# Row sums of a 67 MB array on one Trainium2 core: blocks of 15 rows per partition in place of 16

## The chip, the core and the metric

The kernel runs on one core of one Trainium2 chip. A core has several engines with instruction streams of their own: VectorE (DVE in the profile), ScalarE (ACT), GpSimd (POOL), TensorE (PE, unused here) and SyncE (SP), which here only issues transfers. Transfers between the chip's memory (HBM) and the core's on-chip memory, which has 128 partitions, are carried out by 16 DMA engines that work beside all of these. The metric is the device time of one execution in microseconds (us), the median of several runs. A transfer is issued by SP or by ScalarE, and whoever needs its data waits for its completion signal.

## The reference

The input is x, 32 x 512 x 1024 in float32 (67.11 MB). The output is the sum of each row of 1024 numbers, so 16384 sums:

```python
def reference(x: np.ndarray) -> np.ndarray:
    return np.sum(x, axis=-1).astype(np.float32)
```

## The kernel before

The 16384 rows are dealt out to the 128 partitions, J = 128 rows each. They are cut into eight blocks of 128 x 16 rows (8.39 MB). Within a block, partition p holds 16 rows that are neighbours in memory, so its share is one contiguous run of 64 KB, and the runs of neighbouring partitions lie 64 KB apart. `x_g` (L120) is this view of the input, `out_v` (L121) the same of the output, and `rows_from(j, n)` (L123) picks n rows of a block. The sums are collected in `sums` (L138), 128 columns for each partition.

Buffers for the loaded rows come from the pool `in` (L133), three of them, each of 16 rows and four spare numbers per partition, used in turn. A load into a buffer waits until the work that read its last contents is done. The order of instructions on each engine is the order of the program text (`manual_schedule`, L136).

`rows` (L177) does one load and its reductions: it issues the load on SP (L180), and then sums the rows in one of two ways on VectorE, and the last `n_act` rows on ScalarE. `vec` (L140) is one VectorE instruction for all rows of the load; `halves` (L153), used with `pairs=True`, is one VectorE instruction for each row, which adds the row's two halves and sums up. `act` (L166) sums one row on ScalarE, with an output in another memory that nobody reads.

The order of loads is this. First come 7 rows of the last block (L197 to L200, `FIRST` = 7), the first 7 of its 16. Then come blocks 0 to 6, of 16 rows each (L201 to L208); blocks 0 to 5 are summed by one `vec` each, block 6 by 9 `halves` and 7 `act`. The load of block 1 is held with `hold` (L145, L208) until the reduction of the first 7 rows is done, and as SP issues in order, the loads after it come later too. Then follow the rest of the last block: 6 rows, 2 rows, and its last row in two pieces of 536 and 488 numbers (L210 to L223). The pieces are summed by two `halves`; the first one's sum is placed ahead of the second piece, so that the second instruction adds it in, and a zero written at L220 makes the length even.

Two stores go out. The first, issued by ScalarE (L224), holds the sums of blocks 0 to 6, and is held back until the load of 2 rows has landed. The second, issued by SP (L227), holds the last block's 16 sums of each partition.

Three functions change the finished instruction list, and the change leaves them as they are: `issue_first_load_at_entry` (L10) moves SP's first load to the program's entry, `order_waits` (L31) sorts the waits of single instructions, and `wait_for_the_store_at_the_clear` (L55) lets the last store's wait stand at a later place of the program's end.

Of the kernel before, what the change touches and what calls it, by code (L numbers as in the profile page):

```python
# [100 lines left out]
@with_exitstack  # L101
def kernel(
    ctx: ExitStack,
    tc: tile.TileContext,
    x: bass.AP,
    out: bass.AP,
):
    nc = tc.nc
    nc.at_finalize(issue_first_load_at_entry)
    nc.at_finalize(order_waits)  # L110
    nc.at_finalize(wait_for_the_store_at_the_clear)
    fp32 = mybir.dt.float32
    P = 128
    batch, seq, dim = x.shape
    rows = batch * seq
    J = rows // P
    BIG = 16


    x_g = x.flatten_outer_dims().rearrange("(g p j) d -> g p j d", p=P, j=BIG)  # L120
    out_v = out.rearrange("b s -> (b s)").rearrange("(g p j) -> p g j", p=P, j=BIG)  # L121

    def rows_from(j, n):  # L123
        return x_g[j // BIG, :, j % BIG : j % BIG + n, :]

    last = J // BIG - 1
    FIRST = 7
    pieces = (536, 488)  # L130

    with (
        tc.tile_pool(name="in", bufs=3) as inpool,  # L133
        tc.tile_pool(name="unread", bufs=4, space=bass.MemoryType.PSUM) as upool,
        tc.tile_pool(name="stage", bufs=1) as stpool,
        tc.manual_schedule(),  # L136
    ):
        sums = stpool.tile([P, J], fp32)  # L138

        def vec(dst, src):  # L140
            return nc.vector.tensor_reduce(  # L141
                out=dst, in_=src, axis=mybir.AxisListType.X, op=mybir.AluOpType.add
            )

        def hold(inst, until, reason):  # L145
            tc.add_manual_dep(
                inst.ins,
                until.ins.name,
                mybir.DependencyInfo(mybir.DependencyClass.Sync, mybir.DependencyReason.DATA),
                reason=reason,  # L150
            )

        def halves(dst, src):  # L153
            n = src.shape[-1] // 2
            return nc.vector.tensor_tensor_reduce(  # L155
                out=src[:, :n],
                in0=src[:, :n],
                in1=src[:, n:],
                scale=1.0,
                scalar=0.0,  # L160
                op0=mybir.AluOpType.add,
                op1=mybir.AluOpType.add,
                accum_out=dst,
            )

        def act(dst, src, n):  # L166
            unread = upool.tile([P, dim], fp32)
            nc.scalar.activation(  # L168
                out=unread[:, :n],
                in_=src,  # L170
                func=mybir.ActivationFunctionType.Copy,
                accum_out=dst,
            )

        sums_of = []

        def rows(t, a, n, j, n_act, pairs=False):  # L177
            nv = n - n_act
            block = t[:, a * dim : (a + n) * dim].rearrange("p (n d) -> p n d", d=dim)
            load = nc.sync.dma_start(out=block, in_=rows_from(j, n))  # L180
            if pairs:
                for q in range(nv):
                    sums_of.append(halves(sums[:, j + q : j + q + 1], block[:, q, :]))
            else:
                sums_of.append(vec(sums[:, j : j + nv], block[:, :nv, :]))
            for q in range(nv, n):
                act(sums[:, j + q : j + q + 1], block[:, q, :], dim)
            return load

        def store(eng, g0, g1):  # L190
            return eng.dma_start(
                out=out_v[:, g0:g1],
                in_=sums[:, g0 * BIG : g1 * BIG].rearrange("p (g j) -> p g j", j=BIG),
            )


        j = last * BIG  # L197
        t = inpool.tile([P, BIG * dim + 4], fp32)
        rows(t, 0, FIRST, j, 0)
        first = sums_of[-1]  # L200
        for g in range(last):  # L201
            t = inpool.tile([P, BIG * dim + 4], fp32)
            if g < last - 1:
                load = rows(t, 0, BIG, g * BIG, 0)
            else:
                rows(t, 0, BIG, g * BIG, 7, pairs=True)
            if g == 1:
                hold(load, first, "no descriptors of later loads while the first ones start")  # L208

        t = inpool.tile([P, BIG * dim + 4], fp32)  # L210
        rows(t, FIRST, 6, j + FIRST, 2, pairs=True)
        two = rows(t, FIRST + 6, 2, j + FIRST + 6, 1, pairs=True)
        a = BIG - 1

        j += a
        c, width = pieces
        whole = t[:, a * dim + c : BIG * dim + 2]
        nc.vector.memset(whole[:, width + 1 :], 0.0)  # L220
        part = t[:, a * dim : a * dim + c]
        nc.sync.dma_start(out=part, in_=rows_from(j, 1)[:, 0, :c])  # L222
        nc.sync.dma_start(out=whole[:, 1 : width + 1], in_=rows_from(j, 1)[:, 0, c:])  # L223
        hold(store(nc.scalar, 0, last), two, "its packets come behind those of the loads")  # L224
        halves(whole[:, :1], part)
        halves(sums[:, j : j + 1], whole)
        store(nc.sync, last, last + 1)  # L227


# [28 lines left out]
```

## Time and profile before

| what | value |
|---|---|
| runs, median (lowest, highest) | 161.85 us (161.43, 162.03) |
| span of the profiled execution, first to last instruction | 160.3 us |
| total time of the profiled execution | not recorded; the median lies 1.5 us above its span |
| read from HBM | 67.11 MB, 419 GB/s over the span |
| VectorE: reductions of 16 rows, L141 | 6 of 17.22 us |
| VectorE: reduction of the first 7 rows, L141 | 7.62 us |
| VectorE: one row as halves, L155 | 14 of 0.69 us |
| ScalarE: one row, L168 | 10 of 1.01 us |
| issue of a load on SP, L180 | 0.33 us (median) |
| first load (7 rows), from issue to landing | 11.0 us |

The span is counted from the first to the last instruction, so that what lies around it (starting and finishing the program) belongs to the time of a run, but not to the span. A load's time from issue to landing holds the time that it queues behind other loads. The share of a DMA queue is the time of its packets as a share of what 16 engines have in the span; q1 holds what SP issues, q10 what ScalarE issues. In the chain of work that ended last, each step is followed back to what released it; a step named DMA is the time from a load's issue, or from the end of the piece ahead of it in the chain, to its landing.

### The profile page before, as it was taken

The page shows a single profiled execution, that of the slowest core. Times are in us where ns is not written, and L with a number is a line of the kernel's source. Part 1 is how long each engine was busy: PE and PEld are TensorE (multiplying, and loading weights), DVE is VectorE, ACT ScalarE, POOL GpSimd, SP SyncE. Part 2 cuts the span into 40 slices and gives each one's busy share as a digit, 9 for nine tenths or more (in the row PEclk, how much of TensorE's full clock was granted, in tenths as well). Part 3 has the DMA queues.
Part 4 walks back from the last instruction along what each step waited for, and adds up shares of the span by engine and source line. Part 5 has one row for each costly group of instructions (what it writes and reads, how often), then busy time and mean ns, then how long its engine had stood idle before and what let it go on. Part 6 is the DMA issues. An engine that isn't in the chain of part 4 may idle for free.

```text
span 160.3 us, 132 instructions
## 1 busy us (share of the span) xinstructions
DVE 120.6 (75%) x40; ACT 11.9 (7%) x21; POOL 0.2 (0%) x4
## 2 busy tenths in 40 slices
DVE  0029600499986999679995999949999499994955
ACT  3000000000000000000000000000000000003993
POOL 0000000000000000000000000000000000000000
DMA  8999999899799699699699699796996996996994
GB/s 300 386 491 523 392 392 523 376 409 523 327 458 523 294 491 523 262 523 523 262 523 523 262 523 441 343 523 278 507 523 262 523 523 262 523 523 264 423 384 123
DMA packets 2784, 67.18 MB, mean 419 GB/s; under 512 B 1248, under 2 KB 1376, under 8 KB 1504
## 3 DMA queue, kind: packets, MB, share of 16 engines
q1 hardware_dynamic: 1872, 67.12, 97.7%
q10 hardware_dynamic: 912, 0.06, 0.4%
HBM read 67.11 MB, written 0.07 MB: 419 GB/s over the span
## 4 chain that ended last, share of the span: by engine, by line
DMA 71%; DVE 27%; SPq 1%; issue 0%; DVEq 0%
DMA t<-in_x_dram 71%; DVE sums L141 26%; SPq L180 0%; SPq L222 0%; DVE t L155 0%; DVEq L253 0%
## 5 line engine op out<-in xcount | busy, mean ns | idle before, releaser
L141 DVE TENSOR_REDUCE sums<-t 128x16 f32<-128x16384 f32 (+1 forms) x7 | 110.9, 15848 | 33.8 <-DMA t<-in_x_dram 33.8
L168 ACT ACTIVATE unread<-t 128x1024 f32<-128x1024 f32 x10 | 10.1, 1012 | 145.3 <-DMA t<-in_x_dram 145.3
L155 DVE CUSTOM_DVE_ANT_0 t<-t 128x512 f32<-128x512 f32 (+2 forms) x16 | 9.6, 656 | 4.1 <-DMA t<-in_x_dram 4.0
L168 ACT ACTIVATION_READ_ACCUMULATOR unread<-t 128x1 f32 x10 | 1.9, 187 | 0.0
L168 ACT ACT_TABLE_LOAD x1 | 1.3, 1283 | 0.8 <-PEq L242 0.8
L155 DVE DVE_READ_ACCUMULATOR2_ANT sums<- 128x1 f32 x15 | 1.3, 84 | 0.0
L242 POOL MEMSET const-bfloat16-1.0<- 128x1 bf16 x1 | 0.1, 101 | 0.0
L242 POOL MEMSET const-uint8-127<- 128x1 uint8 x1 | 0.1, 101 | 0.0
L242 POOL MEMSET const-float32-0.0<- 128x1 f32 x1 | 0.1, 98 | 0.2 <-issue 0.2
L242 POOL MEMSET const-float32-1.0<- 128x1 f32 x1 | 0.1, 98 | 0.0
L155 DVE DVE_READ_ACCUMULATOR2_ANT t<- 128x1 f32 x1 | 0.1, 83 | 0.0
L220 DVE MEMSET t<- 128x1 f32 x1 | 0.1, 59 | 0.0
## 6 DMA issues: line engine op xcount, KB each, us to landing
t<-in_x_dram SPq DMA_DIRECT2D x1, 3584.0 KB, 11.0
t<-in_x_dram SPq DMA_DIRECT2D x1, 3072.0 KB, 29.0
t<-in_x_dram SPq DMA_DIRECT2D x1, 1024.0 KB, 31.1
t<-in_x_dram SPq DMA_DIRECT2D x1, 268.0 KB, 31.4
t<-in_x_dram SPq DMA_DIRECT2D x1, 244.0 KB, 31.4
t<-in_x_dram SPq DMA_DIRECT2D x7, 41.1
out_dram<-sums ACTq DMA_DIRECT2D x1, 56.0 KB, 2.1
out_dram<-sums SPq DMA_DIRECT2D x1, 8.0 KB, 1.4
```

The lines of the kernel that those rows point to most:

```text
L141: return nc.vector.tensor_reduce(out=dst, in_=src, axis=mybir.AxisListType.X, op=mybir.AluOpType.add)
L155: return nc.vector.tensor_tensor_reduce(out=src[:, :n], in0=src[:, :n], in1=src[:, n:], scale=1.0, scalar=0.0, op0=mybir.AluOpType.add, op ...
L168: nc.scalar.activation(out=unread[:, :n], in_=src, func=mybir.ActivationFunctionType.Copy, accum_out=dst,)
L220: nc.vector.memset(whole[:, width + 1 :], 0.0)
L242: nc = _bacc.Bacc("TRN2", target_bir_lowering=False, num_devices=1)
```

## The change

Blocks are made of 15 rows for each partition (a run of 60 KB, and runs 60 KB apart), and there are eight of them, for 120 of a partition's 128 rows. The 8 rows that are left form a last block of its own, with runs of 32 KB lying 32 KB apart, loaded as 5 rows, 2 rows and one row in the same two pieces. The early load of 7 rows goes, and with it the hold on block 1's load. Blocks 0 to 6 are summed by one `vec` each, block 7 by 9 `halves` and 6 `act`, the five rows by 4 `halves` and 1 `act`, the two rows by one of each, as they are now. Buffers have 15 rows and no spare numbers. The early store holds 120 sums of each partition, as 8 runs of 60 bytes (it was 7 runs of 64), and the last store 8 (it was 16).

```diff
-    BIG = 16
-    x_g = x.flatten_outer_dims().rearrange("(g p j) d -> g p j d", p=P, j=BIG)
-    out_v = out.rearrange("b s -> (b s)").rearrange("(g p j) -> p g j", p=P, j=BIG)
-    def rows_from(j, n):
-        return x_g[j // BIG, :, j % BIG : j % BIG + n, :]
-    last = J // BIG - 1
-    FIRST = 7
+    BIG = 15
+    blocks = J // BIG
+    REST = J - blocks * BIG
+    assert REST == 8
+    x_r = x.flatten_outer_dims()
+    cut = blocks * P * BIG
+    x_g = x_r[:cut, :].rearrange("(g p j) d -> g p j d", p=P, j=BIG)
+    x_e = x_r[cut:, :].rearrange("(p j) d -> p j d", p=P, j=REST)
+    out_r = out.rearrange("b s -> (b s)")
+    out_g = out_r[:cut].rearrange("(g p j) -> p g j", p=P, j=BIG)
+    out_e = out_r[cut:].rearrange("(p j) -> p j", p=P, j=REST)
     pieces = (536, 488)
...
-        def rows(t, a, n, j, n_act, pairs=False):
+        def rows(t, a, src, j, n_act, pairs=False):
+            n = src.shape[1]
             nv = n - n_act
             block = t[:, a * dim : (a + n) * dim].rearrange("p (n d) -> p n d", d=dim)
-            load = nc.sync.dma_start(out=block, in_=rows_from(j, n))
+            load = nc.sync.dma_start(out=block, in_=src)
...
-        j = last * BIG
-        t = inpool.tile([P, BIG * dim + 4], fp32)
-        rows(t, 0, FIRST, j, 0)
-        first = sums_of[-1]
-        for g in range(last):
-            t = inpool.tile([P, BIG * dim + 4], fp32)
-            if g < last - 1:
-                load = rows(t, 0, BIG, g * BIG, 0)
+        for g in range(blocks):
+            t = inpool.tile([P, BIG * dim], fp32)
+            if g < blocks - 1:
+                rows(t, 0, x_g[g], g * BIG, 0)
             else:
-                rows(t, 0, BIG, g * BIG, 7, pairs=True)
-            if g == 1:
-                hold(load, first, "no descriptors of later loads while the first ones start")
-        t = inpool.tile([P, BIG * dim + 4], fp32)
-        rows(t, FIRST, 6, j + FIRST, 2, pairs=True)
-        two = rows(t, FIRST + 6, 2, j + FIRST + 6, 1, pairs=True)
-        a = BIG - 1
-        j += a
+                rows(t, 0, x_g[g], g * BIG, 6, pairs=True)
+        j = cut // P
+        t = inpool.tile([P, BIG * dim], fp32)
+        rows(t, 0, x_e[:, :5, :], j, 1, pairs=True)
+        two = rows(t, 5, x_e[:, 5:7, :], j + 5, 1, pairs=True)
         c, width = pieces
-        whole = t[:, a * dim + c : BIG * dim + 2]
+        a = 7
+        whole = t[:, a * dim + c : (a + 1) * dim + 2]
...
-        nc.sync.dma_start(out=part, in_=rows_from(j, 1)[:, 0, :c])
-        nc.sync.dma_start(out=whole[:, 1 : width + 1], in_=rows_from(j, 1)[:, 0, c:])
-        hold(store(nc.scalar, 0, last), two, "its packets come behind those of the loads")
+        nc.sync.dma_start(out=part, in_=x_e[:, a, :c])
+        nc.sync.dma_start(out=whole[:, 1 : width + 1], in_=x_e[:, a, c:])
+        early = nc.scalar.dma_start(
+            out=out_g, in_=sums[:, :j].rearrange("p (g j) -> p g j", j=BIG)
+        )
+        hold(early, two, "its packets come behind those of the loads")
         halves(whole[:, :1], part)
-        halves(sums[:, j : j + 1], whole)
-        store(nc.sync, last, last + 1)
+        halves(sums[:, j + a : j + a + 1], whole)
+        nc.sync.dma_start(out=out_e, in_=sums[:, j:])
```

More of the change, by code (lines that the diff above doesn't have):

```diff
@@ L173, in act @@
             )
-        sums_of = []
-        def rows(t, a, n, j, n_act, pairs=False):
+        def rows(t, a, src, j, n_act, pairs=False):
+            n = src.shape[1]
             nv = n - n_act
             block = t[:, a * dim : (a + n) * dim].rearrange("p (n d) -> p n d", d=dim)
-            load = nc.sync.dma_start(out=block, in_=rows_from(j, n))
+            load = nc.sync.dma_start(out=block, in_=src)
             if pairs:
                 for q in range(nv):
-                    sums_of.append(halves(sums[:, j + q : j + q + 1], block[:, q, :]))
+                    halves(sums[:, j + q : j + q + 1], block[:, q, :])
             else:
-                sums_of.append(vec(sums[:, j : j + nv], block[:, :nv, :]))
+                vec(sums[:, j : j + nv], block[:, :nv, :])
             for q in range(nv, n):
@@ L188, in rows @@
             return load
[L190 to L194, printed above, removed]
-        j = last * BIG
-        t = inpool.tile([P, BIG * dim + 4], fp32)
-        rows(t, 0, FIRST, j, 0)
-        first = sums_of[-1]
-        for g in range(last):
-            t = inpool.tile([P, BIG * dim + 4], fp32)
-            if g < last - 1:
-                load = rows(t, 0, BIG, g * BIG, 0)
-            else:
-                rows(t, 0, BIG, g * BIG, 7, pairs=True)
-            if g == 1:
-                hold(load, first, "no descriptors of later loads while the first ones start")
```

## The prediction

> **What bounds the kernel now.** I read the page's busy rows and slices first, then the chain of work that ended last, then busy time by stretches cut at the landings of the loads, then the timeline of the last 12 us.
>
> ```profile
> DVE 120.6 (75%) x40; ACT 11.9 (7%) x21; POOL 0.2 (0%) x4
> DMA  8999999899799699699699699796996996996994
> q1 hardware_dynamic: 1872, 67.12, 97.7%
> q10 hardware_dynamic: 912, 0.06, 0.4%
> DMA 71%; DVE 27%; SPq 1%; issue 0%; DVEq 0%
> ```
>
> No compute engine is full: VectorE has 120.6 of 160.3 us. The load queue q1 has 97.7% of what 16 DMA engines can give in the span. The chain names VectorE for 27%, but only because a load is issued when a reduction frees its buffer; the following table shows that the DMA engines had other loads to work on all the while.
>
> ```profile
> 2.00:11.00 9.00, 0.00 (x0) 0.05 (x1) 0.00 (x0) 1.00 1.10 473
> 11.00:30.34 19.34, 7.62 (x1) 0.00 (x0) 0.00 (x0) 1.00 1.00 434
> 30.34:49.69 19.35, 17.22 (x2) 0.00 (x0) 0.00 (x0) 1.00 1.00 434
> 49.69:69.05 19.36, 17.22 (x2) 0.00 (x0) 0.00 (x0) 1.00 1.00 433
> 69.05:88.54 19.49, 17.22 (x1) 0.00 (x0) 0.00 (x0) 1.00 1.00 430
> 88.54:108.05 19.51, 17.22 (x2) 0.00 (x0) 0.00 (x0) 1.00 1.01 430
> 108.05:127.53 19.48, 17.22 (x1) 0.00 (x0) 0.00 (x0) 1.00 1.00 431
> 127.53:147.06 19.53, 17.22 (x1) 0.00 (x1) 0.00 (x0) 1.00 0.91 396
> ```
>
> Columns: stretch, its length, busy VectorE, ScalarE, GpSimd (instructions), granted clock, DMA share, GB/s (a packet is booked where it starts, so single rows can pass 1.00). Each stretch but the first is one load of 16 rows per partition landing right behind the last: 19.34 to 19.53 us, of which the reduction takes 17.22. So a row per partition (0.524 MB) costs 19.34/16 = 1.209 us at best, 19.53/16 = 1.221 at worst, and 136.06/112 = 1.2148 on the mean of the seven loads. From the seven-row load at 11.0 a start of 11.0 - 7 x 1.209 = 2.5 us follows. The kernel is a start of 2.5 us, 128 rows of DMA, and a tail behind the last byte.
>
> ```profile
> 126.65 31.45 DMA t<-in_x_dram
> 158.09 0.04 issue
> 158.13 0.42 DVE t L155
> 158.54 0.01 DVEq L253
> ```
>
> This is the end of the chain: the last piece lands at 158.09, one short reduction follows, then the store and the end, 2.2 us to the span's end at 160.3. The runs' median is 161.85, so 1.5 us lie outside the span; the change alters nothing there, and the sum below is a difference on the span carried to the median.
>
> **The change part by part.**
>
> Bytes and descriptors. The input is the same 67.11 MB. Loads per partition: before 1 + 7 + 1 + 1 + 2 = 12, after 8 + 1 + 1 + 2 = 12; each partition's part of a load stays one contiguous run (60 KB in place of 64). So a fixed cost per run or per load cancels: 0. SP issues 12 loads in both, at 0.33 to 0.45 us each, beside a stream that is never idle: 0; without that cover the twelve would cost some 4 us in either kernel.
>
> Pitch. Where rows of neighbouring partitions lie 64 KB apart in a full block, they lie 60 KB apart after. All of this trace is read at 64 KB, so the rate at 60 KB is bounded by its rows. If the new pitch made every block as fast as the three fastest, 112 x (1.2148 - 1.209) = 0.65 us would go; the nine rows after 147.06 take 11.07 us to 158.13, and at 1.209 they would take 10.88, 0.2 more: -0.85 in all. If it made all 120 block rows as slow as the slowest load, 120 x (1.221 - 1.2148) = 0.74 us would come. The slower loads start at 69 us while kind, size and pitch of the loads are unchanged, which speaks for a cause that the pitch does not govern; I take the mean rate, 0, and keep -0.85 and +0.74 for the range.
> [...]
>
> Start. The first load grows from 7 to 15 rows, still issued at entry. It lands at 2.5 + 15 x 1.209 = 20.6, VectorE starts 9.6 us later than now, and nobody needs those sums before the early store at 157. The hold goes: the loads of blocks 1 and 2 wait for nothing, and SP issues them within some 2 us of entry, where today the third and fourth load wait to 18.65 (end of the first reduction). For the stream this is 0 if the first packets are not disturbed.
>
> ```profile
> 0.90:1.00 0.10, 0.00 (x0) 0.10 (x1) 0.00 (x0) 1.00 0.94 287
> 1.00:1.10 0.10, 0.00 (x0) 0.10 (x1) 0.00 (x0) 1.00 5.25 1434
> ...
> 1.60:1.70 0.10, 0.00 (x0) 0.10 (x1) 0.00 (x0) 1.00 0.66 287
> 1.70:1.80 0.10, 0.00 (x0) 0.10 (x1) 0.00 (x0) 1.00 0.80 287
> ...
> 1.90:2.00 0.10, 0.00 (x0) 0.10 (x1) 0.00 (x0) 1.00 0.66 287
> ```
>
> These rows (stretches of 0.1 us, GB/s booked at packet starts) show the sixteen engines taking their first packet of 28 KB (287 GB/s over 0.1 us) between 0.9 and 2.0 us, three of them after 1.6. The second load is issued in the same time already, so one issue in the start is in the trace, two more are not. I bound them: at best the first packets gather as early as the early ones (gain under 0.5 us); at worst each of the two adds its issue time of 0.33 us to the last engine, +0.66. I take +0.1, near the low end, since a second issue at this place already left a start of only 2.5 us.
>
> Buffers. After: 9 tiles on 3 buffers. Block g lands at 2.5 + 15(g+1) x 1.2148; the reduction of 15 rows is 15 x 17.22/16 = 16.14 us against 18.2 us between landings, so VectorE has 2.1 us to spare in each block, as now (2.1 to 2.3). A freed buffer's load is issued when one load has about 2 us left and a whole one of 18.2 us is queued behind it: the DMA engines cannot run dry unless a reduction grew by some 20 us. The loads of the last block wait for block 5's reduction: 2.5 + 90 x 1.2148 + 16.14 = 128.0, with block 6 landing at 130.1 and block 7 at 148.3 ahead of them. Cost 0. Behind that wait on SP stand only the other loads of the last block and the last store.
>
> End of the stream. Today, seen back from the end: 16, 6, 2, 1 rows; after: 15, 5, 2, 1. Block 7 lands at 148.3 (one row of 1.2 behind today's 147.06). VectorE takes 9 rows as pairs; today's nine run from 147.06 to 152.65, 5.59/9 = 0.62 us each: 153.9; ScalarE takes 6 at 7.28/7 = 1.04: 154.5. The five rows land where the six do now, 154.34: VectorE 4 x 0.62 = 2.5, to 156.8; ScalarE one row, to 155.6 (from 156.34 now, as it has one row less). Two rows and the two pieces are as today. So the tail carries 0; it has 0.4 us of cover on VectorE before 154.34 and none in the last three microseconds, the same as now.
>
> Stores. The early store goes from 7 x 128 = 896 runs of 64 bytes to 8 x 128 = 1024 of 60, the last from 128 of 64 bytes to 128 of 32.
>
> ```profile
> out_dram<-sums ACTq DMA_DIRECT2D x1, 56.0 KB, 2.1
> out_dram<-sums SPq DMA_DIRECT2D x1, 8.0 KB, 1.4
> ```
>
> The early one is issued at 156.93 and lands at 159.0; the last is issued at 158.58 and lands at 160.0. By runs the early one's packet time (0.4% of 160.3 = 0.64 us an engine) becomes 0.64 x 8/7 = 0.73, +0.1, and 1.0 us of landing time covers it: 0. If 60-byte runs cost twice as much, +0.8, it would still just end under the last store; half in line with it, +0.4 at the worst. The last store is between 0.7 us (half its bytes in half its time) and 1.4: I take 1.4.
> [...]
>
> **Sum.** 0 (bytes, issues, buffers, tail) + 0 (pitch) + 0.1 (start) + 0 (stores): 160.4 us of span, and 161.85 + 0.1 = 161.9 us on the runs' scale. A measurement of this kernel (161.43 to 162.03) tells about 0.5%, 0.8 us, from no change.
>
> **Rivals.**
> *The pitch takes the stretch away.* For it: four of seven loads take 0.15 us more than the rest, so some shared thing slows them; against it: three loads at the same pitch run free. All at 1.209 gives -0.85 and about 161.0; it counts as faster only if nearly all of the stretch goes, or if the runs outside the profile hold more of it.
> *The new pitch is read more slowly.* Place: the eight blocks' packets, 120 x 1.2148 = 145.8 us. For it: no row of the trace was read at 60 KB; against it: runs are as long and as contiguous as before. It decides from 0.81/120 = 0.007 us more a row (18.33 us or more between landings of blocks); at 1% less rate it is +1.5, 163.3 us.
> *The start is disturbed.* Two more loads issued in the first 2 us: +0.66 in place of +0.1, 162.5; it passes 0.8 only if every engine is held for both issues and its first packet restarts. For it: engines already start 1 us apart; against it: the late ones do not show in the first landing.
>
> **Chances and range.** No change, 161.9, own range 161.3 to 162.4: 0.53. Pitch helps: 0.24, of which 0.15 is faster by more than 0.5% and 0.09 within. Pitch hurts: 0.15, all slower. Start: 0.08, half slower, half within. So faster 0.15, within 0.5% 0.53 + 0.09 + 0.04 = 0.66, slower 0.15 + 0.04 = 0.19. The range takes the gain's bound with 0.2 us of the runs' own spread, 160.8, and the loss's bounds of pitch and start together with part of the dearer case, 162.9.
>
> **What will show it.** Right: landings of blocks 18.14 to 18.31 us apart, the first at 20.6, the last piece at 158.0 to 158.4, the reductions 16.1 us with 2 us idle before each, a load queue at 97 to 98%. Pitch helps: all landings at 18.14 and below. Pitch hurts: 18.33 and over in most blocks. Start: first landing after 21.0 with later ones 18.2 apart. I am wrong in the mechanism if a slice of the DMA row in mid-stream is empty, or if VectorE's idle time before a block is gone.

## The result and the profile after

The changed kernel takes 163.44 us (median of 4 runs, 163.09 to 163.49), the kernel before 161.94 (161.43 to 162.22) in the same comparison. The ratio is 1.0096, with a 95% interval of 1.0074 to 1.0118: slower, and outside the predicted range of 160.8 to 162.9. The profiled execution has a span of 161.7 us (total 163.49) against 160.3.

This is busy time by stretches, cut at the landings of the loads, of the changed kernel (stretch, its length, VectorE, ScalarE, GpSimd, clock, DMA share, GB/s):

```profile
21.13:39.25 18.12, 16.16 (x2) 0.00 (x0) 0.00 (x0) 1.00 1.00 434
39.25:57.40 18.15, 16.15 (x2) 0.00 (x0) 0.00 (x0) 1.00 1.00 433
...
111.84:129.99 18.15, 16.16 (x2) 0.00 (x0) 0.00 (x0) 1.00 1.00 433
129.99:148.13 18.14, 16.15 (x2) 0.00 (x1) 0.00 (x0) 1.00 0.96 413
148.13:154.22 6.09, 5.60 (x18) 6.09 (x11) 0.00 (x0) 1.00 0.97 414
```

Every block of 15 rows takes 18.12 to 18.15 us, 1.209 us a row: the rate of before's fastest loads, throughout. The stretch that four loads of before showed (19.5 in place of 19.35) is not there. But the first 15 rows land at 21.13, where 20.6 was worked out. The end of its chain of waits:

```profile
129.34 28.64 DMA t<-in_x_dram
157.98 0.03 issue
158.00 0.42 DVE t L156
158.42 0.01 DVEq L244
```

The last piece lands at 157.98; before, it was 158.09. So at the end of the loads the changed kernel is 0.1 us ahead. Its span ends 1.4 us later all the same. What lies between is the stores; the page's rows of transfers (size, us from issue to landing):

```profile
out_dram<-sums ACTq DMA_DIRECT2D x1, 60.0 KB, 3.9
out_dram<-sums SPq DMA_DIRECT2D x1, 4.0 KB, 2.4
```

Before, these were 2.1 and 1.4. Their issues in the timeline (start, length, ...):

```profile
156.80 0.41 ACTq L212 DMA_DIRECT2D out_dram<-sums  x1
158.46 0.35 SPq L218 DMA_DIRECT2D out_dram<-sums  x1
```

So the early store lands at 160.7, and the last at 160.9, though it has half the bytes. And the list of waits on SP has a row that the kernel before has not:

```profile
SPq L244 <- DMA out_dram<-sums: 1.8, 1, 1.8
```

From the end of the last store's issue at 158.8, SP waits 1.8 us, to 160.7: this is the landing of the early store. The loss of this pair of profiles sits behind the last load.

The pair needs a caution. In every execution with both on record the time of a run is 1.7 to 1.8 us longer than its span, so the span of 160.3 us belongs to an execution of some 162.1, above the median of its runs; in the experiments below the kernel before has a median span of 159.8 to 159.9. Its loads ended late in that one execution (last piece at 158.09; 157.47 and 157.54 in the two profiles below that also read full blocks of 16 rows), and the 0.1 us by which the changed kernel's loads are ahead holds against it alone.

### The profile page after: what moved, and what is told of

Read it like the earlier page. It is cut to its first block, busy times and chain, and to the rows that moved or that the text cites. A ratio compares the mean times of both kernels' runs of the same rounds, so it can differ in the third digit from the quotient of the medians.

```text
span 161.7 us, 129 instructions
## 1 busy us (share of the span) xinstructions
DVE 122.7 (76%) x40; ACT 9.8 (6%) x17; POOL 0.2 (0%) x4
## 4 chain that ended last, share of the span: by engine, by line
DMA 65%; DVE 30%; another core or an unknown queue 1%; SPq 1%; issue 0%; DVEq 0%
DMA t<-in_x_dram 65%; DVE sums L142 30%; SPq L180 0%; SPq L210 0%; DVE t L156 0%; DVEq L244 0%
## 5 line engine op out<-in xcount | busy, mean ns | idle before, releaser
L142 DVE TENSOR_REDUCE sums<-t 128x15 f32<-128x15360 f32 x7 | 113.1, 16154 | 33.1 <-DMA t<-in_x_dram 33.1
L169 ACT ACTIVATE unread<-t 128x1024 f32<-128x1024 f32 x8 | 8.1, 1009 | 147.3 <-DMA t<-in_x_dram 147.3
```

The costliest lines, as they stand in the source:

```text
L142: return nc.vector.tensor_reduce(out=dst, in_=src, axis=mybir.AxisListType.X, op=mybir.AluOpType.add)
L169: nc.scalar.activation(out=unread[:, :n], in_=src, func=mybir.ActivationFunctionType.Copy, accum_out=dst,)
```

## The experiments

Ratios are to the kernel before, run on the same chip in turn (161.55 to 161.69 us there). "The changed kernel" stands at 1.0096. Each edit is against it, unless it says otherwise.

**The stores of before in the changed kernel (`a_store64`).**

```diff
-            out=out_g, in_=sums[:, :j].rearrange("p (g j) -> p g j", j=BIG)
+            out=out_16[:, :7], in_=sums[:, :112].rearrange("p (g j) -> p g j", j=16)
...
-        nc.sync.dma_start(out=out_e, in_=sums[:, j:])
+        nc.sync.dma_start(out=out_16[:, 7:], in_=sums[:, 112:].rearrange("p (g j) -> p g j", j=16))
```

Here `out_16` is the output viewed as before, in groups of 16.

> The changed kernel with the two stores of before: seven runs of 64 bytes per partition early, one of 64 bytes last (the sums go to the places of before's layout, so most land at other rows' places). Theory S (the early store's 60-byte runs land late, 3.9 us after issue against 2.1, and hold up the last store, 2.4 against 1.4): the early store lands in 2.1 us and the last in 1.4, the span falls from 161.7 to 160.2, the time from 163.44 to about 161.9. Rival L (the load stream or the start lost the time): the time stays at 163.4, as no load is touched.

Measured: 161.95 us, ratio 1.0019 (1.0010 to 1.0029), span 160.2. Its rows of the stores:

```profile
out_dram<-sums ACTq DMA_DIRECT2D x1, 56.0 KB, 2.1
out_dram<-sums SPq DMA_DIRECT2D x1, 8.0 KB, 1.4
```

With loads untouched (first reduction at 21.11, last piece at 157.99) the span falls by 1.5 us, and 0.8% of the 0.96% is gone. Theory S holds; a rest of 0.2% (0.3 us) is not in the stores. The landings of the stores are read from one profile for each run; the times are of all its runs.

**The kernel before with 60-byte runs in its early store (`b_store60`).**

```diff
-        hold(store(nc.scalar, 0, last), two, "its packets come behind those of the loads")
+        early = nc.scalar.dma_start(
+            out=out_15, in_=sums[:, :105].rearrange("p (g j) -> p g j", j=15)
+        )
+        hold(early, two, "its packets come behind those of the loads")
```

> The kernel before with one thing of the change: the early store writes seven runs of 60 bytes per partition, lying 60 bytes apart, in place of seven of 64 (the sums of 7 columns are not stored and the others go to other rows' places). Theory S: the early store lands about 3.5 us after issue, the last store about 1 us later than before, the time is about 162.9. Rival L: 161.9 as before. Rival N (it is the eighth run per partition, not the 60 bytes): at most 0.1 us more than before.

Measured: 162.65 us, 1.0069 (1.0054 to 1.0084).

```profile
out_dram<-sums ACTq DMA_DIRECT2D x1, 52.5 KB, 3.4
out_dram<-sums SPq DMA_DIRECT2D x1, 8.0 KB, 1.9
```

Most of the loss from the other side (1.0 us of 1.5): no run more, 3.5 KB less, and the early store lands 1.3 us later. Rival N, the eighth run, is not it, though the eighth adds: 3.4 becomes 3.9 (3.6 to 4.1 in the four profiles with the changed kernel's early store).

**No early store (`a_noearly`).** Its three lines and its `hold` are taken out.

> The changed kernel with its early store left out (120 of 128 sums of each partition are not stored), so that the last store, 128 runs of 32 bytes, is alone. If the last store is late only because the early one's writes are ahead of it: it lands 1.4 us after issue or sooner, and the time is about 161.9 or less. If its own 32-byte runs cost the extra microsecond: it lands at 2.4 us, time 163.4.

Measured: 162.05 us, 1.0027 (1.0018 to 1.0037); the last store, alone, lands in 1.5 us. Its 32-byte runs are not slow; it was late because of the early one.

**What in a 60-byte run costs.** First, 1024 runs of 60 bytes, each placed at a multiple of 64 (`a_run60_at64`), with `out=out_16[:, :, :BIG]` in the early store:

> The changed kernel with its early store's 1024 runs of 60 bytes each placed at a multiple of 64 bytes (so the sums go to other rows' places). Two theories of why the early store lands late. Straddle (runs that lie over a 64-byte boundary cost two writes): the early store lands about 2.1 us after issue, the last about 1.4, time about 162.0, as with 64-byte runs. Partial (a run shorter than 64 bytes is read and written back): it stays at 3.9 and 2.4 us and 163.5.

Measured: the early store lands in 2.8 us, between the two theories. The time (163.28 us, 1.0100) can't be used: the store writes where the last one writes, so the last one was issued only at 159.72, after it had landed. Then it took 1.4 us. Seven such runs, clear of the last store (`a_7run60_at64`, `out_16[:, :7, :BIG]` from `sums[:, :105]`):

> The changed kernel with an early store of seven runs of 60 bytes per partition, each placed at a multiple of 64 bytes (15 columns of sums are not stored, and those stored go to other rows' places); the run before with eight such runs wrote where the last store writes too, so that the last store waited for it and its time said nothing. Straddle theory: the early store lands 2.1 to 2.3 us after issue, the last 1.4, time 162.0. Partial theory: 3.4 and 1.9 us as with seven runs of 60 bytes that lie 60 bytes apart, time about 163.0. By the eight runs' 2.8 us, between 2.1 and 3.9, both have a share: 2.6 us, and the last store 1.4 to 1.5.

Measured: 162.13 us, 1.0034 (1.0021 to 1.0048).

```profile
out_dram<-sums ACTq DMA_DIRECT2D x1, 52.5 KB, 2.6
out_dram<-sums SPq DMA_DIRECT2D x1, 4.0 KB, 1.4
...
SPq L245 <- DMA out_dram<-sums: 0.5, 1, 0.5
```

Placed apart, 60-byte runs cost 0.5 us over 64-byte ones, not the 1.3 of those lying end to end, and the last store is not touched. Then full length, but across boundaries: seven runs of 64 bytes that start 32 bytes past a multiple of 64 (`a_7run64_off32`, the output view starting at element 8):

> The changed kernel with an early store of seven runs of 64 bytes per partition that start 32 bytes behind a multiple of 64 (8 columns of sums are not stored, and those stored go to other rows' places). Each run lies over a boundary, and each is as long as in before. Straddle theory: as late as with 60-byte runs or later, early 3.4 us and more, last 1.9 and more, time 162.7 to 163.3. Partial theory (only the length counts): 2.1 and 1.4, time 162.0.

Measured: 161.98 us, 1.0019 (1.0009 to 1.0029).

```profile
out_dram<-sums ACTq DMA_DIRECT2D x1, 56.0 KB, 2.3
out_dram<-sums SPq DMA_DIRECT2D x1, 4.0 KB, 1.4
```

Lying over a 64-byte boundary costs some 0.2 us here, so straddling alone falls as the main cause. Yet a short run alone is not it either. The two next runs part what is left. The first starts 16 bytes past a multiple of 64 (`a_7run64_off16`):

```diff
+    out_s = out_r[4 : 4 + 7 * P * 16].rearrange("(g p j) -> p g j", p=P, j=16)
...
-            out=out_g, in_=sums[:, :j].rearrange("p (g j) -> p g j", j=BIG)
+            out=out_s, in_=sums[:, :112].rearrange("p (g j) -> p g j", j=16)
```

> The changed kernel with an early store of seven runs of 64 bytes per partition that start 16 bytes past a multiple of 64 (8 columns of sums are not stored, and those stored go to other rows' places). Both ends of each run fall inside a 32-byte unit, which it shares with its neighbour. If it is such ends or such sharing that make the store late: early 3.2 to 3.6 us, last 1.7 to 2.0, time 162.4 to 162.7. If only runs that are not 64 bytes long cost: 2.3 and 1.4, time 162.0, as at an offset of 32.

Measured: 163.02 us, 1.0077 (1.0059 to 1.0095), more than expected.

```profile
out_dram<-sums ACTq DMA_DIRECT2D x1, 56.0 KB, 3.7
out_dram<-sums SPq DMA_DIRECT2D x1, 4.0 KB, 2.4
...
SPq L245 <- DMA out_dram<-sums: 1.6, 1, 1.6
```

The late landing returns almost whole with 64-byte runs, by moving them 16 bytes; in time it is 1.0077 against the 1.0019 of `a_store64` and of the offset of 32. The second run has 52 bytes, 8 past each multiple of 64 (`a_7run52_off8`, `out_16[:, :7, 2:15]` from `sums[:, :91]`): both ends inside a 32-byte unit, none shared.

> The changed kernel with an early store of seven runs of 52 bytes per partition, each 8 bytes past a multiple of 64 (29 columns of sums are not stored, and those stored go to other rows' places). Both ends fall inside a 32-byte unit, but no two runs share one. If the number of such ends counts (one of 60 bytes at a multiple of 64 has one and took 2.6 us): 3.0 to 3.4 us. If sharing counts: 2.6 to 2.8 us. The last store 1.4 to 1.6.

Measured: 162.22 us, 1.0036 (1.0021 to 1.0051).

```profile
out_dram<-sums ACTq DMA_DIRECT2D x1, 45.5 KB, 2.6
out_dram<-sums SPq DMA_DIRECT2D x1, 4.0 KB, 1.4
```

Two ragged ends (ends inside a 32-byte unit) cost no more than the one of `a_7run60_at64`. What the slow runs have beyond that is sharing: the end of one run and the start of the next, written from another partition, fall into one 32-byte unit of the output. With sharing the store of seven runs lands 1.3 to 1.6 us later than 64-byte runs at multiples of 64, with ragged ends alone 0.5 us later. If it is sharing, the unit is 32 bytes, by the offsets of 32 (2.3 us) and 16 (3.7): one of 64 bytes would put the offset of 32 with that of 16, one of 16 bytes the offset of 16 with that of 32.

Sharing fits every row, but two rivals go along with it and no run parts them. A run at an offset of 16, and six of eight of the 60-byte runs lying end to end, also touch three 32-byte units, where all others here of 52 to 64 bytes touch two; and they are ragged and lie over a 64-byte boundary at once, of which the runs above had only one at a time. Runs that do either with gaps between them would tell. Shown is that the placement of the runs makes the store late, not which of the three does it.

**The load side: the hold (`b_nohold`).** The kernel before without its `if g == 1: hold(...)`.

> The kernel before without the hold on block 1's load, so that a third load is issued in the first 2 us. Theory H (more issues in the start pull the engines' first packets apart, which cost the changed kernel about 0.5 us: its first 15 rows landed at 21.1 where 20.6 follows from before): the sixteen engines start their second packets over a stretch of 0.8 us and more in place of 0.5, and the first rows land 0.3 to 0.6 us later, time about 162.3. Rival: the later start of the changed kernel comes from the longer first runs: no change, 161.9.

Measured: 161.64 us, 1.0003 (0.9993 to 1.0012); the first 7 rows land at 10.99 (11.02 with the hold). Theory H falls. The kernel without the hold issues three loads in the first 2 us, as the changed kernel does; with the hold it is two. The run shows something else, too:

```profile
69.03:88.38 19.35, 17.22 (x2) 0.00 (x0) 0.00 (x0) 1.00 1.00 434
88.38:107.72 19.34, 17.21 (x1) 0.00 (x0) 0.00 (x0) 1.00 1.00 434
107.72:127.07 19.35, 17.22 (x1) 0.00 (x0) 0.00 (x0) 1.00 1.00 434
```

These are the stretches that took 19.48 to 19.51 in the profile of before, and at the same pitch of 64 KB they run free; in `b_store60`, with the hold, they take 19.35 too. The last piece of `b_nohold` lands at 157.47.

**The load side: the pitch (`a_pitch64`).** The blocks are read as the first 15 of each 16 rows:

```diff
-    x_g = x_r[:cut, :].rearrange("(g p j) d -> g p j d", p=P, j=BIG)
+    x_g = x_r.rearrange("(g p j) d -> g p j d", p=P, j=16)[:, :, :BIG, :]
```

> The changed kernel, reading its eight blocks of 15 rows at a pitch of 64 KB (the first 15 of each 16 neighbouring rows, so other rows than the reference's are summed); all else as changed. If the pitch removed the stretch of before's later loads (19.5 against 19.35 us for 16 rows): some blocks land 18.3 us apart in place of 18.14, and the last piece lands up to 0.6 us later, time 163.5 to 164.1. If the stretch went for another reason (the hold, the sizes, a quieter chip): landings stay 18.12 to 18.15 us apart and the time is 163.4.

Measured: 163.53 us, 1.0117 (1.0100 to 1.0134), not told apart from the changed kernel.

```profile
20.69:38.95 18.26, 16.15 (x1) 0.00 (x0) 0.00 (x0) 1.00 1.00 431
38.95:57.29 18.34, 16.16 (x2) 0.00 (x0) 0.00 (x0) 1.00 1.00 429
57.29:75.44 18.15, 16.16 (x2) 0.00 (x0) 0.00 (x0) 1.00 1.00 433
```

Two blocks are stretched by 0.1 and 0.2 us, others than in before. Over the runs such stretches came at 64 KB in some executions (0.65 us in before, 0.3 here, none in `b_nohold` and `b_store60`), and blocks read at 60 KB or 480 KB kept their 18.1 us. And the first block lands at 20.69 here, 0.44 earlier than at 60 KB.

**The start (`a_block0_64`, `a_first7`).** In the one, block 0 alone is read at 64 KB; in the other it is loaded as 7 and 8 rows at 60 KB.

```diff
+            if g == 0:
+                x_16 = x_r.rearrange("(g p j) d -> g p j d", p=P, j=16)
+                rows(t, 0, x_16[0, :, :BIG, :], 0, 0)
```

> The changed kernel with block 0 alone read at a pitch of 64 KB (so 15 of each 16 rows there, other rows than the reference's), the stores as changed. If the pitch of the first block sets how late the first rows land (20.7 us at 64 KB, 21.1 at 60 KB in the runs so far): 20.7, later blocks 18.15 apart, and the time falls from 163.45 to about 163.1. If the one landing at 20.7 was chance: 21.1 and 163.4.

```diff
+            if g == 0:
+                rows(t, 0, x_g[0, :, :7, :], 0, 0)
+                rows(t, 7, x_g[0, :, 7:, :], 7, 0)
```

> The changed kernel with block 0 loaded as 7 rows and 8 rows (pitch 60 KB still); the stores as changed. If the late start (the sixteen engines' second packets begin over 1.1 us, and 15 rows land at 21.1) comes from the long first runs: they begin over 0.5 us, 15 rows have landed by 20.7, the time falls from 163.45 to 163.1. If it comes from the pitch: no change, 163.4.

Measured: `a_block0_64` 163.02 us, 1.0088 (1.0074 to 1.0102); `a_first7` 163.25, 1.0098 (1.0085 to 1.0112). This is the timeline (start, length, ...) at the first reduction, of the changed kernel and then of `a_block0_64`:

```profile
21.13 16.15 DVE L142 TENSOR_REDUCE sums<-t 128x15 f32<-128x15360 f32 x1 [21.13 <-DMA t<-in_x_dram]
```

```profile
20.78 16.15 DVE L142 TENSOR_REDUCE sums<-t 128x15 f32<-128x15360 f32 x1 [20.78 <-DMA t<-in_x_dram]
```

Changing the pitch of one block brings 0.35 us of the start back. Eight profiles with 15 rows loaded first at 60 KB have 20.93 to 21.20 here, two at 64 KB 20.69 and 20.78. The time of `a_block0_64` can't be put down to the start alone, as its early store landed in 3.6 us, 0.3 less than the changed kernel's. With `a_first7` 15 rows have landed at 20.93, which a profile with an undivided first load has as well, and its interval overlaps that of the changed kernel: that shorter first runs help is not shown. The windows of the first microseconds show where it lies: second packets of 60 KB (61440 bytes in 0.5 us are 123 GB/s), first in the changed kernel, then in `a_block0_64`:

```profile
3.50:4.00 0.50, 0.00 (x0) 0.00 (x0) 0.00 (x0) 1.00 1.13 492
4.00:4.50 0.50, 0.00 (x0) 0.00 (x0) 0.00 (x0) 1.00 2.55 1106
4.50:5.00 0.50, 0.00 (x0) 0.00 (x0) 0.00 (x0) 1.00 0.85 369
```

```profile
3.50:4.00 0.50, 0.00 (x0) 0.00 (x0) 0.00 (x0) 1.00 0.85 369
4.00:4.50 0.50, 0.00 (x0) 0.00 (x0) 0.00 (x0) 1.00 3.69 1597
4.50:5.00 0.50, 0.00 (x0) 0.00 (x0) 0.00 (x0) 1.00 0.00 0
```

At 60 KB three of sixteen engines begin their second packet after 4.5 us, at 64 KB none. In all eleven profiles with 15 rows loaded at once, the load lands 16.2 to 16.3 us behind the start of the last second packet, which comes at 4.4 to 4.6 us at 64 and 480 KB and at 4.7 to 5.0 at 60. So the late engines are the late landing; how many are late varies (six start after 4.5 us in `a_store64`). The later blocks don't make the lag up: the last piece lands at 157.65 in `a_block0_64`, 0.33 earlier. Why engines start late at this pitch is open.

**A version with long output runs (`c_480`, `c_480_first7`).** Each partition gets 120 neighbouring rows, 15 of them in each block, so that its early sums are one run of 480 bytes:

```diff
-    x_g = x_r[:cut, :].rearrange("(g p j) d -> g p j d", p=P, j=BIG)
+    x_g = x_r[:cut, :].rearrange("(p g j) d -> g p j d", p=P, j=BIG)
-    out_g = out_r[:cut].rearrange("(g p j) -> p g j", p=P, j=BIG)
+    out_g = out_r[:cut].rearrange("(p j) -> p j", p=P)
...
-            out=out_g, in_=sums[:, :j].rearrange("p (g j) -> p g j", j=BIG)
+            out=out_g, in_=sums[:, :j]
```

> The changed kernel with 120 neighbouring rows for each partition instead of 15 in each block (pitch 480 KB, runs of 60 KB as before), so that the early store is 128 runs of 480 bytes. Theory S: fewer and longer runs land quicker, at most 2.1 us for the early store and 1.4 for the last; with the loads at the rate of the 60 KB pitch the time is 161.4 to 162.0. Against it: if a pitch of 480 KB is read more slowly, landings of blocks are over 18.2 us apart and the time above 163.

Measured: 161.77 us, 1.0012 (1.0004 to 1.0021), first 15 rows at 20.80, and

```profile
out_dram<-sums ACTq DMA_DIRECT2D x1, 60.0 KB, 1.6
out_dram<-sums SPq DMA_DIRECT2D x1, 4.0 KB, 1.4
```

The same 60 KB land in 1.6 us instead of 3.9. With block 0 loaded as 7 and 8 rows as well:

> The kernel with 120 neighbouring rows for each partition (early store of 128 runs of 480 bytes), and block 0 loaded as 7 and 8 rows. Splitting block 0 took 0.2 us off the changed kernel (163.45 to 163.25). If that adds to the gain of the long runs: 161.55, level with before (161.55 to 161.6) or just under. If the start at this pitch is no later for long first runs: 161.77 as without the split.

Measured: 161.56 us, 0.9996 (0.9987 to 1.0005): level with the kernel before, and the best version of the change that was found. No run beat the kernel before. In this profile every later block takes 18.14 or 18.15 us, so that only start and tail are left to shorten.

## Why the prediction was wrong

**Where the time lies** was right up to the last load: the load stream bounds the kernel, at 1.209 us a row, and VectorE has 2.0 us to spare in each block (2.1 were worked out). Buffers, issues and the tail up to the last piece cost nothing; it landed at 157.98, where 158.0 to 158.4 was asked for.

**The stores are the step that failed**: "and 1.0 us of landing time covers it: 0". Both halves were wrong, the size of the growth and the cover. The prediction took the early store's growth from its packet time, +0.1 and at most +0.8. The packet time is indeed small (q10 has 0.3% of the span, as against 0.4%), but the landing went from 2.1 to 3.9 us, +1.8. The growth lies behind the packets, as the end of the changed kernel shows (stretch, its length, VectorE, ScalarE, GpSimd, clock, DMA share, GB/s):

```profile
157.70:158.60 0.90, 0.56 (x4) 0.17 (x2) 0.00 (x0) 1.00 0.59 68
158.60:159.20 0.60, 0.00 (x0) 0.00 (x0) 0.00 (x0) 1.00 0.00 0
...
159.50:160.70 1.20, 0.00 (x0) 0.00 (x0) 0.00 (x0) 1.00 0.00 0
```

The early store's packets are over by 158.6, in the kernel before too; there it lands 0.4 us later, here 2.1.

The cover was 0.3 us, not 1.0. The prediction took it as the distance between the two landings (159.0 and 160.0), as though the program ended alike behind each. It does not: in all 16 profiles the span ends 1.0 us behind the landing of the early store or 0.3 behind that of the last, whichever comes later.

| profile | early lands | last lands | early + 1.0 | last + 0.3 | span |
|---|---|---|---|---|---|
| kernel before | 159.0 | 160.0 | 160.0 | 160.3 | 160.3 |
| changed kernel | 160.7 | 160.9 | 161.7 | 161.2 | 161.7 |
| `a_store64` | 158.9 | 159.9 | 159.9 | 160.2 | 160.2 |
| `b_store60` | 159.8 | 159.9 | 160.8 | 160.2 | 160.8 |
| `a_7run60_at64` | 159.3 | 159.8 | 160.3 | 160.1 | 160.3 |
| `a_7run64_off16` | 160.5 | 160.9 | 161.5 | 161.2 | 161.5 |
| `c_480` | 158.1 | 159.6 | 159.1 | 159.9 | 159.9 |

It is the early store, then, that ends the changed kernel: 1.8 us later, less the cover of 0.3, is the 1.5 us of span that `a_store64` takes off. The last store, for which the prediction took 1.4 us ("I take 1.4"), did land later, in 2.4, but this costs nothing of its own, since its path ends at 161.2. A bound from the landing, the quantity that the program's end waits for, would have allowed for its doubling, 2.1 us.

Why the last store is late with the early one: wherever the early one took 3.4 us or more, the last landed 0.1 to 0.4 us behind it (160.7 and 160.9 in the changed kernel, 159.8 and 159.9 in `b_store60`, 160.5 and 160.9 in `a_7run64_off16`), and in 1.4 to 1.5 us where the early one was done or absent. The Trainium skill (DMA: Bandwidth & Descriptors, "Queues, rings and completion order") states that a transfer's completion signal lands only after every earlier write of the same DMA engine, across its queues; these rows agree.

**The start** was mis-sized and its reason wrong. The sum had +0.1 for two more issues; there is one more (three in the first 2 us, where it was two), and `b_nohold` shows that it costs nothing. Measured are about 0.5 (21.13 against 20.6). About 0.35 of it goes with the pitch of the first block, which the prediction did not name; the rest, also there at 64 KB, is open.

**The pitch** term of 0 was right for the median, by the runs: the stretch of before belongs to single executions, since `b_nohold` and `b_store60` read at 64 KB without it. In the pair of profiles its absence is worth 0.65 us, which hides the later start: 0.5 lost, 0.65 gained, the last piece 0.1 us earlier. That the last piece came where the prediction had it is thus luck: two things that its sum did not have cancel in this pair.

**The range** did not follow from its own bounds: 161.85 with the pitch's +0.74 and the start's +0.66 is 163.25, above the 162.9 that was given for the two together, and the stores' +0.4 would make 163.65. That would have held the measured time, though not for its cause.

The rival on the slower side, a slower read at 60 KB, is refuted (434 GB/s). The outcome lay in a term that the prediction took to be covered and for which it named no rival.

## What to carry to other kernels

Bound a store at the end of a kernel by its time to landing, not by its packets: what waits at the end is the landing, and how much of the program stands behind each landing decides which one counts. Before changing a tile's size, look at what it does to the output's runs; here runs that start and end at multiples of 32 bytes, or a layout that gives each partition one long run, kept that landing at 1.6 to 2.3 us in place of 3.9. A stretch seen in one execution is no property of the layout until another execution shows it.

## What the hardware showed unexpectedly

Sixteen bytes of offset moved a 56 KB store from 2.1 us to 3.7, while 32 bytes moved it to 2.3. The first load landed about 0.35 us later at a pitch of 60 KB than at 64 KB, with all later blocks at full rate at either; this was not followed further.
